# Sample retention states of a hybrid decoder layer: from TensorE matmuls on stacked split operands to element-wise passes on GpSimd

## The chip, the cores and the metric

The kernel runs on one core of a Trainium2 chip. The core has TensorE (PE in the profile, its weight loads PEld), VectorE (DVE), ScalarE (ACT), GpSimd (POOL) and SyncE (SP), which here only issues DMAs. Each engine takes its own instructions in the order in which they stand and waits on semaphores for the others. The metric is the device time of one launch in microseconds, as a median of several runs; lower is better.

## The reference, cut to what matters

One layer on 256 prompt tokens and, at the same time, 8 sequences of 8 sample tokens (320 columns in all). RMSNorm and an input projection feed an S5 head group and a retention head group; an output projection, a residual, a second norm and a SwiGLU feed-forward part of width 5632 follow. The change concerns one output of the retention group, the state of each sample sequence after its 8 tokens:

```python
def step(r, inp):
    qc, kc, vc = inp
    ...
    r_new = r * chunk_decay + jnp.einsum('bhmd,bhme->bhde', kc * k_decay, vc)
    return r_new, o
```

For the sample (`b` 8 sequences, `h` 8 heads, `m` 8 tokens, `d` and `e` 128 each) `r_new` is the old state times a scalar of the head plus the sum over 8 tokens of an outer product of a key (scaled by a power of the head's gamma) and a value. In all 64 states of 128x128 fp32, 512 KB per head. Nothing later in the layer reads them.

## The kernel before, in words

All activations lie transposed, features on the 128 partitions and the 320 tokens in columns. Weights are fp32 and are used in two parts: `wload` has SP load a chunk of 8 k-tiles (128x1024, 512 KB) into a tile `raw`, ACT casts it to `hi` (L131) and DVE subtracts, `lo = raw - hi` (L133). `gemm` then does three matmuls per k-tile: hi by x-hi (L143), hi by x-lo (L144), lo by x-hi (L145). Activations are split the same way.

The stages: a mixing stage (input projection, S5 scan, the eight retention heads, until about 340 us), the output projection and the GLU (until 488 us), then the feed-forward stage. That one runs `ffn_in(0)`, `ffn_in(1)`, `ffn_out(0)`, `ffn_in(2)`, `ffn_out(1)`, `ffn_in(3)`, `ffn_out(2)`, `ffn_out(3)`. Each `ffn_in` has 11 blocks (n = 0 to 43 in all) of two gemms of 16 k-tiles, `ps_fg` and `ps_fu`: four weight chunks a block. Behind them DVE scales both results, multiplies them (`fu<-fu,fg`) and makes `alo`.

Buffers: weights use the pool `wp` (3 `raw`, 3 `hi`, 3 `lo`) up to the first gemm of the feed-forward stage, after that `wp2` (4 `raw`, 3 `hi`, 3 `lo`). The state update takes its tiles from `wp`, under the same names, once the weights have left it.

Order: PE and POOL run in the order of the source (`tc.manual_schedule`). SP, ACT and DVE are ordered by the tile scheduler when the kernel is built; weight loads carry a high priority.

The state update before: in the mixing stage `head_k` transposes the sample's keys too and ACT stores them, scaled, in `kv[64:128]`; `head_v` stores the values in `kv[0:64]`. In the feed-forward stage `states_split` makes hi and lo parts of `kv` and stacks them by DMAs from ACT's queue; `states_load(h)` loads a head's old states and has DVE mask the values (`bmk`) so that one matmul serves four sequences; `states_add(h)` does two matmuls (`psu`, L1168) per head, DVE adds them to the scaled old state, and SP stores the result to `rs_o`.

Of the kernel before, what the change touches and what calls it, by code (L numbers as in the profile page):

```python
# [12 lines left out]
F32 = mybir.dt.float32  # L13
F32R = mybir.dt.float32r
# [3 lines left out]
ADD, SUB, MUL = ALU.add, ALU.subtract, ALU.mult  # L18
# [24 lines left out]

@with_exitstack
def hybrid_kernel(ctx, tc, xT, w_in, w_in4, w_out, w_glu, w_fi, w_fo, vecs, s5p, bc, x0,
                  r0, trig, masks, kdec, bmask, gq,
                  yT, s5p_o, s5s_o, rp_o, rs_o):
    nc = tc.nc
    pe, act, dve, pool, sp = nc.tensor, nc.scalar, nc.vector, nc.gpsimd, nc.sync
# [5 lines left out]
    def f(t):  # L55
        return t.bitcast(F32)
# [9 lines left out]
    bmk = cst.tile([P, 4], F32, name="bmk")  # L66

    kv = cst.tile([P, H, P], F32, name="kv")
# [32 lines left out]
    def mm(cost, *a, **k):  # L101
        pe.matmul(*a, **k)
        clk.now += cost

    def tr(out, in_):
        m = in_.shape[0]
        pe.transpose(out, in_, ident[:m, :m])
        clk.now += 0.12
# [68 lines left out]
    def tt(out, a, b, op):  # L177
        dve.tensor_tensor(out, a, b, op)  # L178
# [72 lines left out]
    kdc = mp.tile([P, H, 3], F32, name="kdc")  # L251
    gqt = mp.tile([P, H, NS], F32, name="gqt")
    retp = mp.tile([P, H, N], F32, name="retp")

# [462 lines left out]
    def head_k(h, q_, qg, k_, R):  # L717
        yield DL["k"]
        pst = misc("pst")
        for i, s in enumerate(STARTS):  # L720
            tr(pst[:, P * i:P * i + P], k_[:, s:s + P])
        kd = mp.tile([P, 2, P], F32, name="kd", tag="kd", bufs=1)
        with tc.high_priority(offset=EVAC):
            for i in range(2):
                act.mul(kd[:, i], pst[:, P * i:P * i + P], kdc[:, h, i:i + 1])
            act.mul(kv[64:128, h], pst[64:128, 2 * P:3 * P], kdc[64:128, h, 2:3])
        pss = misc("pss")
        mm(0.43, pss[:, 0:256], k_[:, 0:P], q_[:, 0:256], start=True, stop=True)
# [12 lines left out]

    def head_v(h, v_, qg, rt, R):
# [5 lines left out]
        with tc.high_priority(offset=EVAC):  # L748
            for i in range(3):
                act.mul(vT[:, i], pst2[:, P * i:P * i + P], rtok[:, i:i + 1])  # L750
        last = act.copy(kv[0:64, h], vT[64:128, 2])
        if h == 0:
            rot_t["values"] = last
            with tc.issue_after(last.ins):
# [10 lines left out]
        if h % 2:  # L765
            two = (HS[h - 1], R)
            for g in range(2):
                mm(0.11, po[64 * g:64 * g + 64, 2], smp[:, g], kv[0:64, h - 1 + g], start=True, stop=False,
                   tile_position=(0, 64 * g), skip_group_check=True)
# [103 lines left out]
    def do_k(h, ps=None):  # L873
        ps = proj(9 + 4 * h) if ps is None else ps
        R = HS[h]
        k_ = rot(ps, "k_")
        spawn(head_k(h, R["q_"], R["qg"], k_, R))
        run_due()

# [70 lines left out]
        k0 = k1  # L950
    ps0, ps1, pq, pk = accs
    for t_, s_ in ((x0t, x0), (csr, trig), (kdc, kdec),
                   (bmk, bmask), (gqt, gq)):
        sp.dma_start(t_, s_)
    for c in range(2):
        load_bc(c)
# [55 lines left out]
    def advance():  # L1012
        clk.now = max(clk.now, clk.heap[0][0])
        run_due()
# [52 lines left out]
        split_r(r4b[:, h - 4], h)  # L1067
    while clk.heap:
        advance()
    s5stack.close()  # L1070

    gl = ExitStack()
# [53 lines left out]
    def norm_ps(name):  # L1126
        return ps_n.tile([P, 512], F32, name=name, tag="n", bufs=2)
# [7 lines left out]

    SU = {}

    def states_split():  # L1140
        kvh, kvl = (wp.tile([P, 8, P], F32R, name=n, tag=n, bufs=3) for n in ("hi", "lo"))
        act.copy(kvh, kv)
        tt(kvl, kv, f(kvh), SUB)
        SU["k"] = [wp.tile([P, 8, P], F32R, name="hi", tag="hi", bufs=3) for _ in range(2)]
        SU["v"] = [wp.tile([P, 8, P], F32R, name="lo", tag="lo", bufs=3) for _ in range(2)]
        for i in range(2):
            for a in range(4):
                d = slice(32 * a, 32 * a + 32)
                act.dma_start(f(SU["k"][i][d]), f((kvh, kvl)[a // 2][64 + 32 * i:96 + 32 * i]))
                act.dma_start(f(SU["v"][i][d]), f((kvh, kvl)[a % 2][32 * i:32 * i + 32]))  # L1150

    def states_load(h):
        rt = wp.tile([P, NB, P], F32, name="raw", tag="raw", bufs=3)
        sp.dma_start(rt, r0[h])
        n = ("hi", "lo")[h % 2]
        vm = wp.tile([P, NB, P], F32R, name=n, tag=n, bufs=3)
        with tc.high_priority(offset=EVAC):
            for i in range(2):
                tt(vm[:, 4 * i:4 * i + 4], f(SU["v"][i][:, h]).unsqueeze(1).to_broadcast([P, 4, P]),
                   bmk.unsqueeze(2).to_broadcast([P, 4, P]), MUL)  # L1160
        SU[h] = rt, vm

    def states_add(h):
        rt, vm = SU.pop(h)
        for i in range(2):
            q = slice(4 * i, 4 * i + 4)
            ps = norm_ps("psu")
            pe.matmul(ps, SU["k"][i][:, h], vm[:, q].rearrange("p b e -> p (b e)"), start=True, stop=True)  # L1168
            stt(rt[:, q], rt[:, q], float(GAM[h] ** NS), ps.rearrange("p (b e) -> p b e", e=P), MUL, ADD)
        sp.dma_start(rs_o[h], rt)  # L1170

    def ffn_in(c):
        ahi = fp.tile([P, FCT, N], F32R, name="ahi", tag="ahi", bufs=2)
        alo = fp.tile([P, FCT, N], F32R, name="alo", tag="alo", bufs=2)
        for i in range(FCT):
            n = c * FCT + i
            if n == 0:
                spawn(ffn_norm(), DL["n2"])
            pg = gemm("ps_fg", w_fi[2 * n], KT, hhi, hlo)
            g = fp.tile([P, N], F32, name="fg", tag="fg", bufs=2)  # L1180
            tt(g, pg, rbc2, MUL)
            act.activation(g, g, AF.Silu)
            if n == 0:
                wpool[:] = [wp2, WP2]
            pu = gemm("ps_fu", w_fi[2 * n + 1], KT, hhi, hlo)
            u = fp.tile([P, N], F32, name="fu", tag="fu", bufs=2)
            tt(u, pu, rbc2, MUL)
            tt(u, u, g, MUL)
            act.copy(ahi[:, i], u)
            tt(alo[:, i], u, f(ahi[:, i]), SUB)  # L1190
            if c == 0:
                if i == 0:
                    states_split()
                if 3 <= i:
                    states_add(i - 3)
                if 2 <= i < 2 + H:
                    states_load(i - 2)
        return ahi, alo

    wp2 = ctx.enter_context(tc.tile_pool(name="wp2", bufs=1, reuse_waits="tile"))  # L1200
# [41 lines left out]
def _host(inp):  # L1242
# [58 lines left out]
    kd = np.zeros((P, H, 3))  # L1301
    for i in range(2):
        kd[:, :, i] = gam[None, :] ** (NP - 1 - (P * i + np.arange(P)[:, None])) * sc
    kd[64:, :, 2] = gam[None, :] ** (NS - 1 - (tt_[:, None] % 8)) * sc
    A["kdec"] = kd.astype(f)
    A["bmask"] = c((np.arange(P)[:, None] // 8 % 4 == np.arange(4)[None, :]).astype(f))
    A["gq"] = c(np.broadcast_to((gam[:, None] ** (np.arange(NS) + 1.0))[None], (P, H, NS)).astype(f))
    return A

# [25 lines left out]
```

## Time and profile before

| | |
|---|---|
| median of 3 runs | 1441.32 us (1441.31 to 1441.67) |
| span of the profiled execution | 1438.9 us |
| PE busy | 1425.4 us (99%) |
| DVE, ACT, POOL busy | 847.6, 600.2, 75.1 us |
| HBM read, written | 220.66 MB, 10.26 MB |
| granted TensorE clock, mean | 0.998 |

The span runs from the first to the last instruction of one profiled execution; the runs' times also hold what lies around it. Busy time of an engine is the union of its instructions, and a wait inside an instruction counts as busy. Matmuls are pipelined: a row of 0.31 us is issued every 0.15 us.

### The profile page before, as it was taken

To read this page: it belongs to the slowest core of one execution; us is meant where nothing else is said; L and a number is where in the kernel's file an instruction comes from. 1 tells how busy PE (TensorE), PEld (TensorE's weight loads), DVE (VectorE), ACT (ScalarE), POOL (GpSimd) and SP (SyncE) were. 2 spreads that over 40 slices of the span, in tenths; PEclk is the share of its full clock that TensorE was granted. 3 is DMA by queue.
4 is the path that set the end of the run, shared out by engine and by line. 5 is a ranking of instruction groups with operands and counts; after the bars stand their busy time and mean duration, and the time that the engine had idled before them with its cause. 6 is when DMAs were issued, how large, how long until landed. Compare 5 with 4: busy or idle time off the path is not lost.

```text
span 1438.9 us, 25723 instructions
## 1 busy us (share of the span) xinstructions
PE 1425.4 (99%) x10434; PEld 1411.7 (98%) x10434; DVE 847.6 (59%) x1378; ACT 600.2 (42%) x945; POOL 75.1 (5%) x161
## 2 busy tenths in 40 slices
PE   9999999999999999999999999999999999999997
PEld 8999999999999999999999999999999999999996
DVE  8978787777567655655444444454444444444454
ACT  7645555554355533333333333333333333333452
POOL 7610000000000000000000000000000000000001
PEclk9999999999999999999999999999999999999999
DMA  8555555556544666654444455444445444445443
GB/s 287 167 171 165 158 172 151 173 146 208 173 147 149 209 200 206 214 194 161 148 152 145 127 155 171 156 149 146 125 149 167 162 147 151 146 129 151 152 145 110
DMA packets 92774, 235.09 MB, mean 163 GB/s; under 512 B 26480, under 2 KB 40432, under 8 KB 92656
## 3 DMA queue, kind: packets, MB, share of 16 engines
q1 hardware_dynamic: 91744, 231.09, 50.7%
q10 hardware_dynamic: 912, 2.36, 0.6%
q8 instruction: 82, 1.34, 0.4%
q14 instruction: 36, 0.29, 0.1%
HBM read 220.66 MB, written 10.26 MB: 160 GB/s over the span
## 4 chain that ended last, share of the span: by engine, by line
PE 71%; DVE 1%; ACT 0%; issue 0%; DVEq 0%
PE ps_fo L144 7%; PE ps_fu L144 7%; PE ps_fu L145 7%; PE ps_fo L143 7%; PE ps_fu L143 7%; PE ps_fo L145 7%; PE ps_fg L143 7%; PE ps_fg L144 7%; PE ps_fg L145 7%; PE ps_o L144 1%; PE ps_o L143 1%; PE ps_o L145 1%; PE ps_g L144 1%; PE ps_g L145 1%; PE ps_g L143 1%; DVE x L178 0%
## 5 line engine op out<-in xcount | busy, mean ns | idle before, releaser
L133 DVE TENSOR_TENSOR lo<-raw,hi 128x1024 fp32r<-128x1024 f32 (+1 forms) x416 | 466.9, 1123 | 376.1 <-ACT hi L131 375.1
L131 ACT CAST hi<-raw 128x1024 fp32r<-128x1024 f32 (+1 forms) x416 | 402.0, 967 | 684.7 <-PE ps_fo L144 189.3
L143 PE MATMUL ps_fg<-hhi,hi 128*128 128x320 f32 x704 | 217.6, 309 | 0.0
L144 PE MATMUL ps_fo<-alo,hi 128*128 128x320 f32 x704 | 217.5, 309 | 0.0
L145 PE MATMUL ps_fo<-ahi,lo 128*128 128x320 f32 x704 | 217.5, 309 | 0.0
L143 PE MATMUL ps_fo<-ahi,hi 128*128 128x320 f32 x704 | 217.5, 309 | 0.0
L144 PE MATMUL ps_fg<-hlo,hi 128*128 128x320 f32 x704 | 217.4, 309 | 0.0
L144 PE MATMUL ps_fu<-hlo,hi 128*128 128x320 f32 x704 | 217.4, 309 | 0.0
L143 PE MATMUL ps_fu<-hhi,hi 128*128 128x320 f32 x704 | 217.4, 309 | 0.0
L145 PE MATMUL ps_fu<-hhi,lo 128*128 128x320 f32 x704 | 217.4, 309 | 0.0
L145 PE MATMUL ps_fg<-hhi,lo 128*128 128x320 f32 x704 | 217.4, 309 | 0.0
L143 PE MATMUL ps_p<-xhi,hi 128*128 128x320 f32 x560 | 177.8, 317 | 0.0
L145 PE MATMUL ps_p<-xhi,lo 128*128 128x320 f32 x560 | 173.3, 310 | 0.4 <-DVE lo L133 0.4
L144 PE MATMUL ps_p<-xlo,hi 128*128 128x320 f32 x560 | 172.9, 309 | 0.0
L144 PEld LDWEIGHTS ps_fg<-hlo,hi 128*128 128x128 f32 x704 | 132.4, 188 | 0.4
L143 PEld LDWEIGHTS ps_fg<-hhi,hi 128*128 128x128 f32 x704 | 132.3, 188 | 0.3
L143 PEld LDWEIGHTS ps_fu<-hhi,hi 128*128 128x128 f32 x704 | 132.4, 188 | 0.0
L144 PEld LDWEIGHTS ps_fu<-hlo,hi 128*128 128x128 f32 x704 | 132.4, 188 | 0.0
L145 PEld LDWEIGHTS ps_fu<-hhi,lo 128*128 128x128 f32 x704 | 132.4, 188 | 0.0
L145 PEld LDWEIGHTS ps_fg<-hhi,lo 128*128 128x128 f32 x704 | 132.3, 188 | 0.0
L143 PEld LDWEIGHTS ps_fo<-ahi,hi 128*128 128x128 f32 x704 | 132.2, 188 | 0.0
L144 PEld LDWEIGHTS ps_fo<-alo,hi 128*128 128x128 f32 x704 | 132.2, 188 | 0.0
(420 smaller groups left out, 1904.7 us busy)
## 6 DMA issues: line engine op xcount, KB each, us to landing
raw<-w_fi SPq DMA_DIRECT2D x176, 512.0 KB, 3.7
raw<-w_in SPq DMA_DIRECT2D x79, 512.0 KB, 4.1
raw<-w_fo SPq DMA_DIRECT2D x64, 512.0 KB, 3.5
raw<-w_out SPq DMA_DIRECT2D x32, 512.0 KB, 3.7
raw<-w_fo SPq DMA_DIRECT2D x64, 192.0 KB, 2.4
rt<-r SPq DMA_DIRECT2D x8, 512.0 KB, 5.4
raw<-w_glu SPq DMA_DIRECT2D x8, 512.0 KB, 3.4
raw<-r SPq DMA_DIRECT2D x8, 512.0 KB, 4.3
```

Of the source, the lines that this page charges most:

```text
L131: cast = act.copy(hi[:, :m], raw[:, :m])
L133: dve.tensor_tensor(lo[:, :m], raw[:, :m], f(hi[:, :m]), SUB)
L143: pe.matmul(ps, hi, xhi[:, k], start=k == 0, stop=False)
L144: pe.matmul(ps, hi, xlo[:, k], start=False, stop=False)
L145: pe.matmul(ps, lo, xhi[:, k], start=False, stop=k == nk - 1)
```

## The change

The sample's keys are no longer transposed. After each head's rotation POOL multiplies them by powers of gamma (`kdt`) into `kvf` (features on partitions, one column per token). The values stay token by token in `vs`, and eight DMAs at the end of the mixing stage write them to a DRAM tile `vd`, so that `vd[h, t]` is 8 sequences x 128 values of token t, 4 KB. The update is cut into 64 steps, one per head and token. A step loads `vd[h, t]` to all 128 partitions (`vb`, a 512 KB broadcast load into a buffer named `hi`), POOL multiplies it by the token's key column (`kvt`, named `lo`, 128x1024) and adds it to the state (named `raw`, 128x1024). Once per head POOL scales the state by a constant first. The source issues two steps per block of `ffn_in` from n = 2 on, with the load two steps ahead of its use.

```diff
@@ mixing stage
-        for i, s in enumerate(STARTS):
-            tr(pst[:, P * i:P * i + P], k_[:, s:s + P])
+        for i in range(2):
+            tr(pst[:, P * i:P * i + P], k_[:, P * i:P * i + P])
...
-            act.mul(kv[64:128, h], pst[64:128, 2 * P:3 * P], kdc[64:128, h, 2:3])
...
-        last = act.copy(kv[0:64, h], vT[64:128, 2])
+        last = act.copy(vs[:, h], vT[64:128, 2])
...
         k_ = rot(ps, "k_")
+        pool.tensor_tensor(kvf[:, h], k_[:, NP:N].rearrange("p (b t) -> p b t", t=NS),
+                           kdt[:, h].unsqueeze(1).to_broadcast([P, NB, NS]), MUL)
...
     while clk.heap:
         advance()
+    for b in range(NB):
+        sp.dma_start(vd[:, :, b].rearrange("h t e -> t h e"), vs[NS * b:NS * b + NS])
@@ feed-forward stage
-    def states_split():
...
-    def states_load(h):
...
-    def states_add(h):
...
+    SU = {"n": 0, "loads": []}
+
+    def states_load(j):
+
+        h, t = divmod(j, NS)
+        if t == 0:
+            SU["rt"] = wp.tile([P, NB, P], F32, name="raw", tag="raw", bufs=3)
+            sp.dma_start(SU["rt"], r0[h])
+        vb = wp.tile([P, NB, P], F32, name="hi", tag="hi", bufs=3)
+        sp.dma_start(vb, vd[h, t].unsqueeze(0).to_broadcast([P, NB, P]))
+        SU["loads"].append((h, t, vb, SU["rt"]))
+
+    def states_add():
+        h, t, vb, rt = SU["loads"].pop(0)
+        if t == 0:
+            pool.tensor_scalar(rt, rt, float(GAM[h] ** NS), None, MUL)
+        kvt = wp.tile([P, NB, P], F32, name="lo", tag="lo", bufs=3)
+        pool.tensor_tensor(kvt, vb, kvf[:, h, :, t].unsqueeze(2).to_broadcast([P, NB, P]), MUL)
+        pool.tensor_tensor(rt, rt, kvt, ADD)
+        if t == NS - 1:
+            sp.dma_start(rs_o[h], rt)
+
+    def states_step():
+        j = SU["n"]
+        SU["n"] += 1
+        if j < H * NS:
+            states_load(j)
+        if 2 <= j < H * NS + 2:
+            states_add()
...
-            if c == 0:
-                if i == 0:
-                    states_split()
-                if 3 <= i:
-                    states_add(i - 3)
-                if 2 <= i < 2 + H:
-                    states_load(i - 2)
+            if n >= 2:
+                states_step()
+                states_step()
```

How the scheduler orders SP's queue around it shows in the built programs. First SP in `ffn_in(0)` of the kernel before, a piece from the first state store on. `raw<-w_fi` is a weight chunk, `raw<-r0` a head's old states; in brackets are the engines or DMA queues that a row waits for.

```order
L1170 DMA rs_o<-raw_6810 128x1024 [waits DMAHW1_49,DVE_49]
L130 DMA raw_7169<-w_fi 128x1024 [waits DMAHW5_49,DMAHW2_49,DVE_49]
L1154 DMA raw_7236<-r0 128x1024 [waits DMAHW1_49]
L130 DMA raw_7241<-w_fi 128x1024 [waits DMAHW6_49,DVE_49]
L130 DMA raw_7247<-w_fi 128x1024 [waits DMAHW7_49,DVE_49]
L130 DMA raw_7305<-w_fi 128x1024 [waits DMAHW0_49,DVE_49]
L1170 DMA rs_o<-raw_6952 128x1024 [waits DVE_49]
```

There two state transfers of a head stand among four weight chunks, and all wait for DVE or DMA queues. The same engine in the changed kernel, from weight chunk 8 of the feed-forward stage (counted from 0) on; `hi<-vd` is a broadcast load:

```order
L130 DMA raw_6660<-w_fi 128x1024 [waits DMAHW6_49,DMAHW2_49,DVE_49]
L1152 DMA hi_6792<-vd_77 128x1024 [waits DMAHW3_49,PE_49]
L1152 DMA hi_6794<-vd_77 128x1024 [waits PE_49]
L130 DMA raw_6666<-w_fi 128x1024 [waits DMAHW7_49,DVE_49]
L1152 DMA hi_6926<-vd_77 128x1024 [waits PE_49]
L130 DMA raw_6724<-w_fi 128x1024 [waits DMAHW0_49,DVE_49]
L1152 DMA hi_6932<-vd_77 128x1024 [waits DMAHW3_49,Pool_49]
L130 DMA raw_6730<-w_fi 128x1024 [waits DMAHW1_49,DVE_49]
L1152 DMA hi_7067<-vd_77 128x1024 [waits DMAHW4_49,DMAHW2_49,Pool_49]
L130 DMA raw_6796<-w_fi 128x1024 [waits DVE_49]
```

From the fourth on, each broadcast load waits for POOL, and a weight load stands behind it; so it goes on to the 64th. The end of that piece on SP in the changed kernel, where the 64 loads run out:

```order
L1152 DMA hi_12665<-vd_77 128x1024 [waits DMAHW4_49,DMAHW2_49,Pool_49]
L130 DMA raw_8835<-w_fi 128x1024 [waits DVE_49]
L1152 DMA hi_12670<-vd_77 128x1024 [waits DMAHW6_49,Pool_49]
L130 DMA raw_8841<-w_fi 128x1024 [waits DMAHW5_49,DVE_49]
L130 DMA raw_8911<-w_fi 128x1024 [waits DMAHW7_49,DVE_49]
L1163 DMA rs_o<-raw_11487 128x1024 [waits Pool_49]
L130 DMA raw_8917<-w_fi 128x1024 [waits DMAHW1_49,DMAHW0_49,DVE_49]
```

The store of the last head stands two weight chunks behind the last broadcast load, before chunk 73; 62 weight loads stand between the first and the last of the 64. And POOL in the changed kernel at the start of the steps, where the kernel before has nothing between the last head's norm and the closing passes over `x1`:

```order
L1158 TENSOR_SCALAR raw_6790<-raw_6790 128x1024 [waits DMAHW4_49,DMAHW3_49,DMAHW5_49,DMAHW2_49,DMAHW6_49,DMAHW1_49,DMAHW7_49,DMAHW0_49,DVE_49]
L1160 TENSOR_TENSOR lo_6929<-hi_6792,kvf_74 128x1024 [waits DMAHW3_49,PE_49]
L1161 TENSOR_TENSOR raw_6790<-raw_6790,lo_6929 128x1024 [waits Pool_49]
L1160 TENSOR_TENSOR lo_6934<-hi_6794,kvf_74 128x1024 [waits DMAHW4_49,DVE_49,PE_49]
L1161 TENSOR_TENSOR raw_6790<-raw_6790,lo_6934 128x1024 [waits Pool_49]
```

Two passes of 128x1024 a step, 64 times, each addition behind its product. After the first few steps POOL waits only for the broadcast loads and its own results.

More of the change, by code (lines that the diff above doesn't have):

```diff
@@ L45, in hybrid_kernel @@
 def hybrid_kernel(ctx, tc, xT, w_in, w_in4, w_out, w_glu, w_fi, w_fo, vecs, s5p, bc, x0,
-                  r0, trig, masks, kdec, bmask, gq,
+                  r0, trig, masks, kdec, kdf, gq,
                   yT, s5p_o, s5s_o, rp_o, rs_o):
@@ L65, in hybrid_kernel @@
     vec = cst.tile([P, vecs.shape[1]], F32, name="vec")
-    bmk = cst.tile([P, 4], F32, name="bmk")
-    kv = cst.tile([P, H, P], F32, name="kv")
+    kvf = cst.tile([P, H, NB, NS], F32, name="kvf")
+    drs = ctx.enter_context(tc.tile_pool(name="drs", bufs=1, space=bass.MemoryType.DRAM))
+    vd = drs.tile([H, NS, NB, P], F32, name="vd")
     voff = {}
@@ L250, in hybrid_kernel @@
     csr = mp.tile([P, 2, N], F32, name="csr")
-    kdc = mp.tile([P, H, 3], F32, name="kdc")
+    kdc = mp.tile([P, H, 2], F32, name="kdc")
+    kdt = mp.tile([P, H, NS], F32, name="kdt")
+    vs = mp.tile([64, H, P], F32, name="vs")
     gqt = mp.tile([P, H, NS], F32, name="gqt")
@@ L767, in head_v @@
             for g in range(2):
-                mm(0.11, po[64 * g:64 * g + 64, 2], smp[:, g], kv[0:64, h - 1 + g], start=True, stop=False,
+                mm(0.11, po[64 * g:64 * g + 64, 2], smp[:, g], vs[:, h - 1 + g], start=True, stop=False,
                    tile_position=(0, 64 * g), skip_group_check=True)
@@ L952, in hybrid_kernel @@
     for t_, s_ in ((x0t, x0), (csr, trig), (kdc, kdec),
-                   (bmk, bmask), (gqt, gq)):
+                   (kdt, kdf), (gqt, gq)):
         sp.dma_start(t_, s_)
@@ L1133, in ffn_norm @@
         act.copy(rbc2, next(rg))
-    SU = {}
-    def states_split():
[L1141 to L1150, printed above, removed]
@@ L1152, in states_load @@
-    def states_load(h):
[L1153 to L1161, printed above, removed]
-    def states_add(h):
[L1164 to L1170, printed above, removed]
+    SU = {"n": 0, "loads": []}
@@ L1300, in _host @@
     A["masks"] = c(np.concatenate([mk, np.concatenate([sm, np.zeros_like(sm)], 1)], 2).astype(f))
-    kd = np.zeros((P, H, 3))
+    kd = np.zeros((P, H, 2))
     for i in range(2):
         kd[:, :, i] = gam[None, :] ** (NP - 1 - (P * i + np.arange(P)[:, None])) * sc
-    kd[64:, :, 2] = gam[None, :] ** (NS - 1 - (tt_[:, None] % 8)) * sc
     A["kdec"] = kd.astype(f)
-    A["bmask"] = c((np.arange(P)[:, None] // 8 % 4 == np.arange(4)[None, :]).astype(f))
+    A["kdf"] = c(np.broadcast_to((gam[:, None] ** (NS - 1.0 - np.arange(NS)) * sc)[None], (P, H, NS)).astype(f))
     A["gq"] = c(np.broadcast_to((gam[:, None] ** (np.arange(NS) + 1.0))[None], (P, H, NS)).astype(f))
```

## The prediction

> **What bounds the kernel now.** I read the page first (engine totals and the chain that ended last), then stretches of the feed-forward stage, then single rows of ACT, DVE and the queues there.
>
> ```profile
> span 1438.9 us, 25723 instructions
> PE 1425.4 (99%) x10434; PEld 1411.7 (98%) x10434; DVE 847.6 (59%) x1378; ACT 600.2 (42%) x945; POOL 75.1 (5%) x161
> PE 71%; DVE 1%; ACT 0%; issue 0%; DVEq 0%
> 660.00:810.00 150.00, 150.00 (x1024) 150.00 (x1024) 72.02 (x88) 53.21 (x65) 0.00 (x0) 1.00 0.45 144
> 1425.00:1438.00 13.00, 3.26 (x17) 2.38 (x16) 6.25 (x22) 0.43 (x1) 4.14 (x5) 0.78 0.51 202
> ```
>
> The last two are stretches: length, then busy time of PE, weight loads, DVE, ACT and POOL, granted clock, DMA share, GB/s. In the feed-forward stage PE never stops: 1024 matmuls in 150 us, 0.1465 us each. One weight chunk (8 k-tiles, 24 matmuls) is 3.516 us. POOL does nothing there, and DVE is half free.
>
> So only two things count: what leaves PE, and whether the weights still come every 3.516 us. A chunk comes by an SP load into `raw`, an ACT cast to `hi` and a DVE subtraction to `lo`:
>
> ```profile
> 659.35 1.05 ACT L131 CAST hi<-raw 128x1024 fp32r<-128x1024 f32 x1 [2.10 <-issue]
> 660.43 1.23 DVE L133 TENSOR_TENSOR lo<-raw,hi 128x1024 fp32r<-128x1024 f32 x1 [2.29 <-ACT hi L131]
> 663.50 0.49 DVE L178 TENSOR_TENSOR fu<-fu,fg 128x320 f32<-128x320 f32 x1
> 665.09 0.49 DVE L178 TENSOR_TENSOR alo<-fu,ahi 128x320 fp32r<-128x320 f32 x1
> raw<-w_fi SPq DMA_DIRECT2D x176, 512.0 KB, 3.7
> rt<-r SPq DMA_DIRECT2D x8, 512.0 KB, 5.4
> SPq L130 <- DVE lo L133: 973.4, 384, 7.5
> ```
>
> From issue to use that is 3.7 + 1.05 + 1.23 = 6.0 us. The last row is the queue's own: 384 times SP stood at a weight load until DVE had freed a `raw` buffer. SP runs ahead only as far as the buffers go, and whatever stands behind a waiting load waits too.
>
> **What PE is spared.**
>
> ```profile
> 546.62 0.46 PE psu L1168 x2
> 648.39 0.46 PE psu L1168 x2
> L107 PEld LDWEIGHTS pst<-ident,k__729 x3: 138/138/140, 52.5 to 52.8; 128*128 128x128 f32 x3
> 488.47 1.06 ACT hi L1142
> 489.55 1.23 DVE lo L178
> 491.35 0.31 PE L145 MATMUL ps_fg<-hhi,lo 128*128 128x320 f32 x1
> 491.79 0.80 PE L102 MATMUL ps_r<-ones,acc 128*128 128x1 f32 x6
> ```
>
> The first two rows are the first and last of eight such pairs on the chain: 8 x 0.46 = 3.7 us go. Of each head's three transposes of k one goes: 8 x 0.14 = 1.1 us. Between 491.50 (a matmul's 0.15 after the start of the row at 491.35) and 491.79 PE stands until the norm's sum is there, behind the cast and subtraction of `kv` (L1142 and after it, rows of the chain); 0.3 us go. Together 5.1 us. The DVE passes that go (masks and additions) and eight ACT multiplications are worth nothing: PE works through them.
>
> **What is added beside other work.** Eight small POOL products `kvf` in the mixing stage (POOL is busy 5% of the span) and eight stores to `vd` some 150 us ahead of their use: nothing, as long as POOL has room. `k_` has one buffer; were POOL full there, the next head's rotation would wait.
>
> **The 64 steps.** SP's order in the changed kernel decides. Its first two broadcast loads stand behind weight chunk 8 (counted from 0), and from the first to the last of the 64 there are only 62 weight loads: one `vb` per chunk, not one per two as the source reads. `vb` j goes into the buffer of `vb` j-3, so SP waits there until POOL has done product j-3, and the next weight load stands behind it. POOL's order has two passes of 128x1024 per step and waits for nothing on PE. So from a few steps on, one chunk comes per POOL step of T us. After the last `vb` come two more weight loads, then the store of head 7, which waits for POOL's very last addition, and behind it chunk 73.
>
> No row shows a POOL pass of that size. The nearest:
>
> ```profile
> L504 POOL TENSOR_TENSOR e<-e,ecs 128x128 f32<-128x128 f32 x1 | 0.4, 432 | 0.0
> L504 POOL TENSOR_TENSOR e<-e,ecs 128x256 f32<-128x256 f32 x1 | 0.6, 647 | 0.0
> L1236 POOL TENSOR_TENSOR x<-x,acc 128x320 f32<-128x320 f32 x5 | 4.1, 868 | 1101.9 <-ACT acc L1231 1101.9
> L325 POOL MEMSET d<- 128x512 f32 x2 | 1.0, 528 | 0.0
> L325 POOL MEMSET xp<- 128x640 f32 x2 | 1.2, 634 | 0.0
> ```
>
> The product has one repeated operand like L504, which grows by 215 ns per 128 columns: 647 + 6 x 215 = 1.94 us. The addition is in place on two full operands like L1236: in proportion 868 x 3.2 = 2.78 us, on the line through 128x128 2.47; I take 2.6, near the row of its own form. A pass thus lies between 1.94 and 2.78. The scaling, once in eight steps, has one input: 0.95 us at the memsets' slope, 2.6 as an addition; I take 1.3, an eighth of it 0.16.
>
> By the Trainium skill, GPSIMD Engine Reference, section 3.1, a two-input fp32 pass over 2048 columns takes 4497 ns; half of that, an estimate from that page, would be 2.25 a pass, and the sum below 1582 instead of 1585.
>
> Does POOL run freely beside DVE? Rows of the mixing stage:
>
> ```profile
> 59.11 1.21 DVE L133 TENSOR_TENSOR lo<-raw,hi 128x1024 fp32r<-128x1024 f32 x1
> 59.22 1.23 POOL L515 TENSOR_TENSOR tabl<-tabl,ta 128x32 f32<-128x32 f32 x1
> 61.10 0.27 POOL L518 TENSOR_TENSOR tabl<-tabl,ta 128x32 f32<-128x32 f32 x1
> 69.38 1.08 POOL L455 TENSOR_TENSOR scrt<-x0t,lp 128x256 f32<-128x256 f32 x1
> 69.89 1.65 DVE L133 TENSOR_TENSOR lo<-raw,hi 128x1024 fp32r<-128x1024 f32 x1
> 70.54 1.60 POOL L456 TENSOR_TENSOR lx<-scrt 128x256 f32<-128x256 f32 x1
> 71.46 1.22 DVE L178 TENSOR_TENSOR m<-raw_bc,lpc 128x512 f32<-128x512 f32 x1
> ```
>
> It doesn't. The same 128x32 POOL operation takes 0.27 us alone and 1.23 issued just after a `lo`. Then four in turn: `lo`, issued at 69.89, ends at 71.54, 1.08 after L455 ended; L456 ends at 72.14, 0.60 after `lo`; `m` at 72.68, 0.54 after L456. They take turns, each whole, and 1.23 - 1.08 = 0.15 of an operation's own time hides in the wait. For passes four times as wide no row shows it; I take it as the same.
>
> By the Trainium skill, SBUF — State Buffer, "Who interferes with whom", a DVE instruction with two SBUF inputs and a POOL instruction that reads SBUF exclude each other for the whole instruction, whatever its width; these rows agree at 256 columns.
>
> So while PE starves, each step holds POOL up by one `lo` (1.08) and half of the two small products per block of four chunks (0.49 - 0.15 = 0.34 each, 0.17 per step). Between dependent POOL operations lie 0.08 us (70.46 to 70.54 above).
>
> T = 1.94 + 2.6 + 0.16 + 0.08 + 1.08 + 0.17 = 6.03 us. Bounds: both passes 1.94 and the scaling 0.95, 5.33; both 2.78 and 2.6, 7.22.
>
> **The sum.**
>
> ```profile
> 497.17 0.31 PE L143 MATMUL ps_fu<-hhi,hi 128*128 128x320 f32 x1
> 497.47 1.23 DVE L133 TENSOR_TENSOR lo<-raw,hi 128x1024 fp32r<-128x1024 f32 x1 [0.29 <-ACT hi L131]
> ```
>
> PE began chunk 2 at 497.17, so chunk 73 is due at 497.17 + 71 x 3.516 = 746.8. The second row is `lo` of chunk 4; its end, 498.70, lets SP load chunk 8 and then `vb` 0, which lands 3.7 to 5.4 us later: POOL starts at about 503.4. It ends at 503.4 + 64T, and 6.0 us later chunk 73 is ready. The delay is 64T - 237.4. With 6.03 that is 148.5 us: span 1438.9 - 5.1 + 148.5 = 1582.3. The profiled span is 2.4 us under the median of the runs, 1441.3, so the time is 1585. The bounds of T give 1540 and 1661.
>
> **Rivals.**
> - *No exclusion between such wide passes.* T = 4.78, delay 68.5: 1505. Against it stand the rows above; for it, that they are narrower.
> - *The clock falls.* With T = 6.03 PE works 3.5 us and stands 2.5 in each step. The granted clock is 1.00 while PE is busy and 0.78 in the idle end (the stretch from 1425). At half clock a chunk takes 7.03 us and PE itself paces: from chunk 18, where the starving begins, to 72, 55 x 1.0 = 55 more: 1640. The Trainium skill, TensorE: Matmul & The Clock Gate, "What's actually happening", has the clock halved after an idle window of about 3.4 us; by that rule the 2.5 us stand would leave it full, while a T above 6.9 would not.
> - *The broadcast load is slow.* It reads one 4 KB row 128 times; no row shows such a load. The nearest of its size land in 3.7 and 5.4 us, and from the release of a buffer to its next use lie 2.5T = 15 us. Beyond that it paces: 20 us would make T 8 and the time 1711.
> - *Faster.* Were two-input passes as quick as memsets, 0.95 each, T would be 1.9 + 0.12 + 0.08 + 1.25 = 3.35, under a chunk's 3.516; SP would never be late and the 5.1 us stay: 1436. This decides below T = 3.71, where 64T is 237.4. Every two-input row above is dearer.
>
> **How the numbers follow.** The forecast (turns taken, T within its bounds) has 0.76, no exclusion 0.10, the falling clock 0.05, the slow load 0.05, the faster case 0.04. A range of 1500 to 1650 holds nearly all of the first and the next two; the two last and the uppermost end of T lie outside. Changes under 0.2% (2.9 us) can't be told from none: faster 0.04, within it 0.01 (T just at its turning point), slower 0.95.
>
> **What the next profile would show.** `psu` rows gone. PE solid until about 553 us: `vb` j lets chunk 8 + j be used at 493.3 + 6.03j, due at 518.3 + 3.516j, equal at j = 10. From there to about 895 PE busy for 3.516 of 6.03, digits of 5 or 6; the last 15 us of it one stop (the store of head 7); solid again after, with POOL idle. POOL busy about 75 + 64 x 6 = 455 us, since its rows count the wait for DVE. SP's longest waits at L1152 and on POOL. `lo` rows above 1.23 us while POOL works. Wrong: the passes' length above all, a microsecond per step moving the time by 64; then whether turns are taken; then SP not held where its order has it.

## The result, and the profile after

The changed kernel takes 1571.45 us (median; 1570.05 to 1573.48) against 1441.32 us: a ratio of 1.0902, 95% interval 1.0889 to 1.0915. The forecast was 1585 us, range 1500 to 1650.

The page of the kernel after: totals, then busy tenths in 40 slices of 39.3 us, then the chain that ended last by engine and by line.

```profile
span 1571.7 us, 25855 instructions
PE 1461.3 (93%) x10410; PEld 1432.2 (91%) x10410; DVE 964.4 (61%) x1345; ACT 597.2 (38%) x936; POOL 445.0 (28%) x305
PE   9999999999999976776878799999999999999997
POOL 7510010100000999999999200000000000000001
PEclk9999999999999998999989899999999999999999
...
PE 48%; POOL 23%; DMA 1%; DVE 1%; issue 0%; ACT 0%; SPq 0%; DVEq 0%; POOLq 0%; ACTq 0%
```

Counted from 0, TensorE now has a hole from slice 14 to slice 22, and POOL is solid from slice 13 to slice 21. POOL, which was not on the chain before, is 23% of it.

Two stretches of the same trace (length; busy time of PE, weight loads, DVE, ACT, POOL; granted clock; DMA share; GB/s):

```profile
600.00:700.00 100.00, 75.48 (x434) 71.01 (x433) 69.52 (x37) 22.66 (x27) 98.67 (x38) 0.91 0.66 217
900.00:1000.00 100.00, 100.00 (x684) 100.00 (x683) 46.60 (x61) 33.58 (x43) 0.00 (x0) 1.00 0.45 141
```

The matmuls have the same shape in both; the second is the end of `ffn_in(1)` and a part of `ffn_out(0)`. Beside POOL's steps there are 434 matmuls in 100 us, one chunk of 24 in 5.53 us; after them 684, one in 3.51.

Who holds the weights up is in SP's own queue, and what POOL does in its rows (minimum, median and maximum of a duration in ns, first and last start):

```profile
SPq L130 <- DVE lo L133: 778.0, 317, 7.5
SPq L1152 <- POOL lo L1160: 224.9, 54, 5.8
SPq L1163 <- POOL raw L1161: 69.4, 8, 17.3
```

```profile
L1160 POOL TENSOR_TENSOR lo<-hi,kvf x64: 1904/2897/2906, 510.0 to 870.1; 128x1024 f32<-128x1024 f32 x64
L1161 POOL TENSOR_TENSOR raw<-raw,lo x64: 2337/2520/3272, 512.7 to 872.1; 128x1024 f32<-128x1024 f32 x64
L1158 POOL TENSOR_SCALAR raw<-raw x8: 2768/3628/3748, 488.1 to 828.8; 128x1024 f32<-128x1024 f32 x8
```

The first row is no sign of trouble: the kernel before, whose TensorE never stops, has 973.4 us of it, SP running ahead of free buffers. The other two, waits for POOL, are new. SP stood 54 times at a broadcast load (L1152) until POOL had done a product, and 8 times at a store (L1163) until an addition was done. From the first addition's start to the last one's lie 872.1 - 512.7 = 359.4 us, 5.70 for each of 63 steps; this is T, the length of a POOL step. The broadcast loads of L1152 themselves, from issue to landing:

```profile
DMA to landing us min/median/max: 3.6/4.3/7.5
```

The groups of POOL's rows (busy us, mean ns of one) say of what a step is made:

```profile
L1161 POOL TENSOR_TENSOR raw<-raw,lo 128x1024 f32<-128x1024 f32 x64 | 169.8, 2653 | 5.0
L1160 POOL TENSOR_TENSOR lo<-hi,kvf 128x1024 f32<-128x1024 f32 x64 | 167.8, 2621 | 19.0 <-DMA hi<-vd 19.0
L1158 POOL TENSOR_SCALAR raw<-raw 128x1024 f32<-128x1024 f32 x8 | 27.1, 3392 | 158.0 <-DMA raw<-r 157.8
```

2.62 for a product, 2.65 for an addition and 27.1/64 = 0.42 for the scaling's share make 5.70 with unrounded means: POOL does nothing else in these 360 us.

The end of the stretch, in the chain of the kernel after (start, length, what):

```profile
872.06 2.35 POOL raw L1161
...
874.42 0.34 SPq L1163
...
874.87 5.11 DMA raw<-w_fi
...
880.08 1.05 ACT hi L131
...
881.15 1.24 DVE lo L133
```

The last addition ends, SP issues the store of head 7, and only then the weight load behind it; TensorE gets its chunk after another 5.11 + 1.05 us. Its row there (in brackets the idle time ahead of it):

```profile
881.18 0.63 PE L143 MATMUL ps_fg<-hhi,hi 128*128 128x320 f32 x1 [9.11 <-ACT hi L131]
```

### The profile page after: what moved, and what is told of

Read it like the earlier page. It is cut to its first block, busy times and chain, and to the rows that moved or that the text cites. A ratio compares the mean times of both kernels' runs of the same rounds, so it can differ in the third digit from the quotient of the medians.

```text
span 1571.7 us, 25855 instructions
## 1 busy us (share of the span) xinstructions
PE 1461.3 (93%) x10410; PEld 1432.2 (91%) x10410; DVE 964.4 (61%) x1345; ACT 597.2 (38%) x936; POOL 445.0 (28%) x305
## 4 chain that ended last, share of the span: by engine, by line
PE 48%; POOL 23%; DMA 1%; DVE 1%; issue 0%; ACT 0%; SPq 0%; DVEq 0%; POOLq 0%; ACTq 0%
POOL raw L1161 11%; POOL lo L1160 11%; PE ps_fo L145 7%; PE ps_fo L143 7%; PE ps_fo L144 7%; PE ps_fu L145 4%; PE ps_fu L143 4%; PE ps_fu L144 4%; PE ps_fg L145 4%; PE ps_fg L143 4%; PE ps_fg L144 4%; POOL raw L1158 2%; PE ps_o L143 1%; PE ps_o L144 1%; PE ps_o L145 1%; DMA raw<-w_fi 1%
## 5 line engine op out<-in xcount | busy, mean ns | idle before, releaser
L133 DVE TENSOR_TENSOR lo<-raw,hi 128x1024 fp32r<-128x1024 f32 (+1 forms) x416 | 556.9, 1339 | 436.2 <-ACT hi L131 435.8
L145 PE MATMUL ps_fu<-hhi,lo 128*128 128x320 f32 x704 | 224.4, 319 | 32.4 <-DVE lo L133 32.0
L145 PE MATMUL ps_fg<-hhi,lo 128*128 128x320 f32 x704 | 225.7, 321 | 28.3 <-DVE lo L133 28.3
L143 PE MATMUL ps_fg<-hhi,hi 128*128 128x320 f32 x704 | 224.7, 319 | 21.9 <-ACT hi L131 21.8
L143 PE MATMUL ps_fu<-hhi,hi 128*128 128x320 f32 x704 | 222.3, 316 | 10.4 <-ACT hi L131 10.4
L144 PE MATMUL ps_fg<-hlo,hi 128*128 128x320 f32 x704 | 223.2, 317 | 0.0
L1160 POOL TENSOR_TENSOR lo<-hi,kvf 128x1024 f32<-128x1024 f32 x64 | 167.8, 2621 | 19.0 <-DMA hi<-vd 19.0
L1161 POOL TENSOR_TENSOR raw<-raw,lo 128x1024 f32<-128x1024 f32 x64 | 169.8, 2653 | 5.0
L145 PEld LDWEIGHTS ps_fg<-hhi,lo 128*128 128x128 f32 x704 | 137.7, 196 | 33.8 <-DVE lo L133 33.8
L143 PEld LDWEIGHTS ps_fg<-hhi,hi 128*128 128x128 f32 x704 | 137.6, 196 | 23.8 <-ACT hi L131 23.7
L144 PEld LDWEIGHTS ps_fg<-hlo,hi 128*128 128x128 f32 x704 | 137.8, 196 | 0.0
```

The lines of the kernel that those rows point to most:

```text
L133: dve.tensor_tensor(lo[:, :m], raw[:, :m], f(hi[:, :m]), SUB)
L143: pe.matmul(ps, hi, xhi[:, k], start=k == 0, stop=False)
L144: pe.matmul(ps, hi, xlo[:, k], start=False, stop=False)
L145: pe.matmul(ps, lo, xhi[:, k], start=False, stop=k == nk - 1)
L1160: pool.tensor_tensor(kvt, vb, kvf[:, h, :, t].unsqueeze(2).to_broadcast([P, NB, P]), MUL)
L1161: pool.tensor_tensor(rt, rt, kvt, ADD)
```

## Experiments

The runs have labels, e1 to e11, which the expectations use too. The theory: SP issues in order, has one broadcast load for each weight chunk, and waits at each for POOL; so a chunk comes once in a POOL step. Rivals: A, POOL's passes shut VectorE out and its low parts come late; B, the traffic of the broadcast loads delays the weights; C, TensorE's falling clock.

### The floor: the states left out, and the passes narrowed

Run e3 leaves out the states; what remains is called the floor.

```diff
             if n >= 2:
-                states_step()
-                states_step()
+                pass
```

> Edit: the sample states are left out of the feed-forward stage altogether (no old states loaded, no broadcast loads, no POOL passes, no store of the sample states); the extra tiles of the mixing stage stay. Every theory: the floor. By the prediction's sum 1441.3 - 5.1 = 1436; by the trace after, in which the feed-forward stage begins at 495.79 instead of 491.79 us, 1441.3 - 5.1 + 4.0 = 1440. What e1 and e2 have above this run is what is left of the sample states' cost.

Measured: 1438.34 us, ratio 0.9978 (0.9969 to 0.9987).

Run e4 keeps all transfers and narrows POOL's passes to one of eight sequences.

```diff
-            pool.tensor_scalar(rt, rt, ...)
+            pool.tensor_scalar(rt[:, 0:1], rt[:, 0:1], ...)
-        pool.tensor_tensor(kvt, vb, kvf[:, h, :, t]...)
-        pool.tensor_tensor(rt, rt, kvt, ADD)
+        pool.tensor_tensor(kvt[:, 0:1], vb[:, 0:1], kvf[:, h, 0:1, t]...)
+        pool.tensor_tensor(rt[:, 0:1], rt[:, 0:1], kvt[:, 0:1], ADD)
```

> Edit: POOL's scaling, product and addition work on one of the eight sequences (128x128 instead of 128x1024), the other seven are stored as loaded; every load, store and place in SP's order is as in the changed kernel. Theory: POOL's step falls to about a fifth (two passes of some 0.3 to 0.5 us and gaps), below the 3.52 us of a weight chunk, so the waits for POOL end and the time is 1440, range 1436 to 1450. Rival B (traffic of 64 broadcast loads of 512 KB beside the weights): all bytes are still moved, one to a weight chunk, so most of the 130 us stays, 1500 or more. Rival A (exclusion) would fall away here too, so e1 and e2 tell A from the theory, and this run tells B.

Measured: 1438.26 us, ratio 0.9978 (0.9969 to 0.9988). A stretch of it, and one of POOL's groups:

```profile
600.00:700.00 100.00, 100.00 (x684) 100.00 (x683) 48.67 (x57) 35.86 (x43) 34.63 (x59) 1.00 0.94 330
```

```profile
L1161 POOL TENSOR_TENSOR raw<-raw,lo 128x128 f32<-128x128 f32 x64 | 34.0, 531 | 5.0
```

The DMA engines are 94% busy at 330 GB/s, more than the 217 of the kernel after, and TensorE does its full 684 matmuls. Rival B is out: all bytes are moved here, at no cost. Everything above 1438.3 us comes from the length of POOL's passes.

### The length of a step

Three runs shorten POOL's step. Run e5 halves the addition.

```diff
-        pool.tensor_tensor(rt, rt, kvt, ADD)
+        pool.tensor_tensor(rt[:, 0:4], rt[:, 0:4], kvt[:, 0:4], ADD)
```

> Edit: POOL's addition works on four of the eight sequences (128x512 instead of 128x1024), so the other four keep the scaled old state; everything else is as in the changed kernel. Theory (SP in order: one POOL step per weight chunk): the addition falls by about half of 2.34 to 2.65 us, a step by 1.2 to 1.3 us, to 4.4 to 4.5 us, still above 3.52, so the time falls by 64 x 1.2 to 1.3 = 77 to 83 us, to about 1491 (range 1480 to 1505). Rival A (VectorE shut out by POOL's passes sets the pace by itself): the passes shut out a quarter less, and with SP free e2 lost 58 us over the floor to it; the time would go to 1438 + 0.75 x 133 = 1538. Rival C (falling clock as an own term): the half-clock stretches of about 65 us would go as a whole once TensorE's stands get shorter, on top of the steps: 1470 or less.

Measured: 1499.53 us, ratio 1.0397 (1.0381 to 1.0413).

Run e11 leaves out the scaling.

```diff
-        if t == 0:
-            pool.tensor_scalar(rt, rt, float(GAM[h] ** NS), None, MUL)
```

> Edit: the eight scaling passes are left out (the old states are added to as loaded); loads, stores, products, additions and SP's order stay. It sizes the term that the prediction put at 0.16 us a step (64 x 0.16 = 10 us). Theory: seven of the eight passes lie in POOL's chain of steps (the first runs before it, at 488.1 us), 24.3 us together in the trace after, so the time is 1571.5 - 24 = 1547, range 1540 to 1554. Rival (the prediction's size of the term): 1571.5 - 10 = 1561. Rival A (the scaling's time is VectorE's turn taken, given back as waits of the passes beside it): 1565 or more.

Measured: 1552.75 us, ratio 1.0766 (1.0748 to 1.0784).

Run e10 leaves out the products.

```diff
-        kvt = wp.tile([P, NB, P], F32, name="lo", tag="lo", bufs=3)
-        pool.tensor_tensor(kvt, vb, kvf[:, h, :, t]..., MUL)
-        pool.tensor_tensor(rt, rt, kvt, ADD)
+        pool.tensor_tensor(rt, rt, vb, ADD)
```

> Edit: the products are left out; POOL scales the old states and adds the broadcast values to them as loaded, 64 additions of 128x1024; the loads, the stores and SP's order stay in kind, one broadcast load to a weight chunk. Theory (SP in order, the step against the 3.52 us of a weight chunk, turning point at 3.71 us by the prediction's line): a step is one addition of 2.4 to 2.7 us, 0.08 us of gap and 0.34 to 0.45 us for the scaling's share, 2.8 to 3.2 us, below the turning point, so the time is the floor plus little: 1440, range 1437 to 1450. Rival A (VectorE shut out sets the pace without SP): half of e2's passes at one to each weight chunk, so about half of its 58 us stay, 1467. Rival D (the time follows POOL's total work in a line without a turning point, 133 us for 364 us of steps): a step of 3.0 us is 53% of 5.69, so 1438 + 0.53 x 133 = 1508.

Measured: 1451.83 us, ratio 1.0063 (1.0046 to 1.0079).

The additions of the three, each in its own trace: half width, without scaling, and alone.

```profile
L1161 POOL TENSOR_TENSOR raw<-raw,lo x64: 1261/2141/2160, 510.9 to 794.8; 128x512 f32<-128x512 f32 x64
```

```profile
L1159 POOL TENSOR_TENSOR raw<-raw,lo x64: 2339/2523/3322, 508.5 to 849.8; 128x1024 f32<-128x1024 f32 x64
```

```profile
L1159 POOL TENSOR_TENSOR raw<-raw,hi x64: 2394/2644/3494, 507.7 to 745.6; 128x1024 f32<-128x1024 f32 x64
```

With the addition alone, this is TensorE's wait in the feed-forward stage (us in total, times, longest), and these are POOL's groups:

```profile
PE ps_fu L145 <- DVE lo L133: 9.6, 7, 2.1
```

```profile
L1159 POOL TENSOR_TENSOR raw<-raw,hi 128x1024 f32<-128x1024 f32 x64 | 182.4, 2851 | 52.3 <-DMA hi<-vd 48.5
L1158 POOL TENSOR_SCALAR raw<-raw 128x1024 f32<-128x1024 f32 x8 | 28.2, 3525 | 157.9 <-DVE lo L133 157.7
```

| kernel | T, last start minus first, by 63 | 64T - 237.4 | measured above 1438.3 |
|---|---|---|---|
| after | 5.70 | 127.7 | 133.1 |
| without scaling | 5.42 | 109.3 | 114.4 |
| half addition | 4.51 | 51.0 | 61.2 |
| addition alone | 3.78 | 4.3 | 13.5 |

The time follows the prediction's line from 5.70 to 4.51 us: 71.9 us less for 1.20 us of T, 60 to the microsecond where the line has 64, and 18.7 less for 0.29, 65 to the microsecond. So C is no term of its own while the steps last: the half addition's stretch has a granted clock of 0.97 instead of 0.91, and nothing beyond the step's shortening came back.

```profile
600.00:700.00 100.00, 86.18 (x539) 81.54 (x538) 67.12 (x45) 30.00 (x36) 98.20 (x49) 0.97 0.84 272
```

The half addition didn't become half as long (median 2.14 for 2.52 us: most of its rows hold a wait for VectorE), and the step still fell by 1.20, since the products waited less (2.30 in the mean for 2.62). The addition alone lies beyond the turning point: its passes and scalings take 182.4 + 28.2 = 210.6 us, 3.3 to a step, less than a chunk, and the 3.78 is the chunk's pace plus stops. It missed its range by 2 us. TensorE waited for VectorE alone there, seven times and 2.1 us at most. Behind the longest of these stops, which ends at 683.66, is this row:

```profile
680.23 3.38 DVE L133 TENSOR_TENSOR lo<-raw,hi 128x1024 fp32r<-128x1024 f32 x1
```

Its `hi` was ready by 678.65, and a low part takes 1.23 us undisturbed. That is rival A in small: neither its 1467 nor the line without a turning point (1508).

### SP's queue

Run e1 holds each pair of steps behind the last weight load of its block; `last_w` is a new one-element list.

```diff
-                sp.dma_start(raw[:, :m], src[:, k0:k0 + m])
+                last_w[0] = sp.dma_start(raw[:, :m], src[:, k0:k0 + m])
...
-                states_step()
-                states_step()
+                with tc.issue_after(last_w[0].ins):
+                    states_step()
+                    states_step()
```

> Edit: the loads, products and stores of the sample states are the same, but on SP each pair of broadcast loads is held behind the last weight load of its own block, so that two broadcast loads come to four weight loads (14.06 us of TensorE work) instead of one to one. Theory (SP in order waits for POOL at each broadcast load, one step of 5.69 us for one weight chunk of 3.52 us): a pair of steps takes 2 x 5.69 = 11.4 us and has 14.06 us, so SP no longer stops and TensorE runs through; 1441.3 - 5.1 (matmuls and transposes spared) + 4 (the feed-forward stage begins 4 us later than before) = 1440, range 1436 to 1448. Rival A (POOL's passes shut VectorE out, and VectorE's low parts come late for TensorE): POOL makes the same passes, so the time stays near 1571, with low parts above 2 us and TensorE waiting for them. Rival B (the broadcast loads' 33.5 MB delay the weights): the same bytes spread over twice the time, 1500 or more. Rival C (the halved clock alone): clock windows vanish only if TensorE's stands do, so this run does not tell C from the theory.

Measured: 1448.67 us, ratio 1.0047 (1.0032 to 1.0062), 0.7 us over the range. SP's and TensorE's waits, and a stretch:

```profile
SPq L1153 <- POOL lo L1161: 5.3, 6, 1.4
```

```profile
PE ps_fu L146 <- DVE lo L134: 6.7, 7, 1.0
```

```profile
600.00:700.00 100.00, 97.95 (x662) 96.90 (x661) 83.74 (x57) 34.13 (x41) 76.89 (x29) 1.00 0.66 230
```

The same 64 steps of the same passes, only two to four weight chunks: SP's 224.9 us of waiting at broadcast loads are 5.3, and 122.8 of the 133 us are gone. But the edit does two things: SP no longer stands, and POOL's passes lie further apart (busy 76.9 of 100 us instead of 98.7). So it rules out traffic and the passes' mere number, but does not part the theory from rival A; the next run does. Of the 10.3 us left, 6.7 are seven stops of TensorE for a low part; two of them, which end at 631.9 and 689.8 us, come right behind stretches in which POOL worked without a gap from 609.1 and 666.9 us on.

Run e2 issues the transfers of the states from POOL's own queue.

```diff
-            sp.dma_start(SU["rt"], r0[h])
+            pool.dma_start(SU["rt"], r0[h])
-        sp.dma_start(vb, vd[h, t]...)
+        pool.dma_start(vb, vd[h, t]...)
-            sp.dma_start(rs_o[h], rt)
+            pool.dma_start(rs_o[h], rt)
```

> Edit: the broadcast loads, the loads of the old states and the stores of the new ones are issued from POOL's own queue; SP carries weights alone. Theory: POOL now waits for itself only, SP never stands behind it: 1440, range 1436 to 1450, with POOL's steps closer to each other than one to a weight chunk or not, without effect on TensorE; what the issues cost on POOL lengthens POOL's stretch alone. Rival A (exclusion of VectorE by POOL's passes): still near 1571, TensorE waiting on low parts. Rival B (traffic): 64 broadcast loads at the same or a higher rate, still 1500 or more.

Measured: 1496.55 us, ratio 1.0382 (1.0366 to 1.0397). The theory had 1440. A stretch, TensorE's longest wait in sum, and three VectorE operations by their durations in ns:

```profile
600.00:700.00 100.00, 85.71 (x568) 83.08 (x567) 99.71 (x48) 28.97 (x36) 97.81 (x55) 1.00 0.69 228
```

```profile
PE ps_fu L145 <- DVE lo L133: 40.6, 33, 2.0
```

```profile
L178 DVE TENSOR_TENSOR fg<-ps_fg,rbc x21: 475/478/480, 514.8 to 845.7; 128x320 f32<-128x320 f32 x21
L178 DVE TENSOR_TENSOR fu<-fu,fg x22: 494/1692/2445, 504.4 to 849.9; 128x320 f32<-128x320 f32 x22
L178 DVE TENSOR_TENSOR alo<-fu,ahi x22: 2197/2200/2694, 509.0 to 854.5; 128x320 fp32r<-128x320 f32 x22
```

SP is free of POOL here, and the chunks come at 568 matmuls per 100 us instead of 434; but VectorE shows 99.7 of 100 us busy with 48 instructions, since its rows count the time for which POOL holds it up. The operation with one input in PSUM takes its 0.48 us as ever; the two of the same width with both inputs in SBUF take 1.69 and 2.20 in the median, where they took 0.49 before the change. So freeing SP alone takes 74.9 of the 133 us back, with POOL as dense as before; 58 stay. That is rival A, true in kind: a second limit behind the first. POOL's passes packed without a gap leave VectorE too few turns, and TensorE waits for low parts. Whether it is the passes or the issues on POOL, the next run, e7, tells; its edit is that of this run and the narrow passes above together.

> Edit: as in e2 all loads and stores of the sample states are issued from POOL's queue, and as in e4 POOL's passes work on one of eight sequences (128x128). It tells what cost e2 its 58 us over the floor. If it is the passes (VectorE cannot start its own two-input instructions on SBUF while a POOL pass of 1.9 to 2.9 us runs, is 99.8 of 100 us busy or held, and TensorE waits for low parts): the passes here take 0.5 to 0.6 us, the time is the floor, 1438 to 1441. If it is the issue on POOL (80 issues of 0.58 us) or the traffic of this queue: 1460 to 1496.

Measured: 1439.88 us, ratio 0.9984 (0.9975 to 0.9993). Beside narrow passes the issues and the queue cost 1 to 2 us at most; so the 58 us of the run before belong to the passes.

### The last store

Run e6 moves the store of the last head.

```diff
-        if t == NS - 1:
+        if t == NS - 1 and h < H - 1:
             sp.dma_start(rs_o[h], rt)
+        SU["end"] = rt
...
     ffn_out(0, a0)
+    sp.dma_start(rs_o[H - 1], SU["end"])
```

> Edit: only the store of head 7's states is moved, from its place in SP's queue during the feed-forward stage to one after the first output part of that stage; the 64 broadcast loads stay where they are. Theory: the stop of 9.1 us at 871.5 to 881.2 us, in which SP waits for the last addition with a weight load behind it, goes or shrinks to the weight chunk's own chain: 1571.5 - 9 = 1562, range 1559 to 1567. Rival: the last broadcast loads stand there too and hold SP just as long: 1571.

Measured: 1556.84 us, ratio 1.0795 (1.0781 to 1.0810), 14.6 under the kernel after. It isn't the clean test it was meant to be: at that place of the program the steps had reached head 4 (not 5, as the next expectation says), the moved line stored head 4's tile, early, and head 7's states weren't stored. So a second run, e9, holds the right store behind a late weight load; it keeps the first piece above and sets `last_w` as in e1:

```diff
     a3 = ffn_in(3)
+    with tc.issue_after(last_w[0].ins):
+        sp.dma_start(rs_o[H - 1], SU["end"])
```

> Edit: head 7's store alone is held behind the last weight load of the stage's fourth input part, so that it leaves its place in SP's queue (behind the last broadcast loads); the 64 broadcast loads, the other seven stores and their places stay. (In e6 the scheduler took the moved line early, with head 5's tile, and head 7's states were not stored at all.) Theory: of the stop of 9.1 us at 871.5 to 881.2 us the part goes that SP spends at the store, and the last weight loads go out as soon as their own buffers are free: 1571.5 - 9 = 1562, range 1556 to 1567. Rival: the last broadcast loads hold SP just as long, 1571.

Measured: 1559.65 us, ratio 1.0817 (1.0801 to 1.0833), 11.8 less than the kernel after. Its stretch at the end of POOL's work, and the same of the kernel after:

```profile
870.00:900.00 30.00, 29.14 (x199) 28.88 (x198) 17.36 (x19) 10.78 (x13) 1.43 (x1) 1.00 0.48 158
```

```profile
870.00:900.00 30.00, 20.53 (x128) 19.86 (x127) 11.56 (x14) 8.52 (x10) 4.32 (x3) 0.83 0.55 193
```

TensorE's stop is gone from it: 71 matmuls more, which at 0.1465 us each are 10.4 us of work. That is the stop of 9.1 us and the slow start behind it, at a granted clock of 0.83 in the stretch instead of 1.00. The cause of the last 1.4 us stays open.

### The steps spread out

Run e8 spreads the steps, one to a block.

```diff
             if n >= 2:
-                states_step()
-                states_step()
+                with tc.issue_after(last_w[0].ins):
+                    states_step()
...
+            if c < FCH - 1 and n % 2:
+                with tc.issue_after(last_w[0].ins):
+                    states_step()
             tt(x1[:, n], x1[:, n], ps, ADD)
```

The first piece is in `ffn_in`, the second in `ffn_out`; `last_w` is set as above.

> Edit: as e1, but one step (one broadcast load, one product, one addition) to a block of four weight loads in place of two, and 24 of the 66 steps to every second of the first 48 blocks of the output part; each broadcast load behind the last weight load of its block. Theory: a step of 5.5 us has 14 us (10 us in the output part), SP does not wait, and VectorE is shut out by two passes only before it has a free stretch to catch up, where e1 had seven stops of 1.0 to 1.3 us at the third pass or later: floor of e3 plus little, 1438 to 1442, not slower than the kernel before. Rival A (each step costs TensorE a stop of its own of 0.2 us or more): 1438 + 64 x 0.2 = 1451 or more.

Measured: 1439.36 us, ratio 0.9981 (0.9972 to 0.9990), 1 us above the floor. A stretch, and all that TensorE waited for low parts in the feed-forward stage:

```profile
600.00:700.00 100.00, 100.00 (x684) 100.00 (x683) 69.70 (x57) 35.94 (x43) 35.20 (x15) 1.00 0.60 198
```

```profile
PE ps_fo L146 <- DVE lo L134: 0.9, 1, 0.9
```

The whole work of the change is in it, and it is as fast as a kernel without the states to within 1 us. Against the kernel before it gains 0.19%, just about what can be told from none.

## Why the prediction was right, point by point

**One broadcast load per weight chunk, and SP waiting in order.** Right, and it carries the result: with the passes unchanged and only their loads' places in SP's order moved, 122.8 of 133 us went (e1). Freeing SP without spreading the passes takes 74.9 of them (e2); the rest needs the passes apart as well.

**A chunk per step of T.** Right: the line 64T - 237.4 gives 127.7 for the measured T, and 133.1 were measured above the floor. **T itself** was 0.33 us too large, 6.03 for 5.70. Rows of the kernel after show its terms free of VectorE (the last two) and beside it (the first two):

```profile
863.87 2.89 POOL L1160 TENSOR_TENSOR lo<-hi,kvf 128x1024 f32<-128x1024 f32 x1
866.85 3.26 POOL L1161 TENSOR_TENSOR raw<-raw,lo 128x1024 f32<-128x1024 f32 x1
870.07 1.92 POOL L1160 TENSOR_TENSOR lo<-hi,kvf 128x1024 f32<-128x1024 f32 x1
872.06 2.34 POOL L1161 TENSOR_TENSOR raw<-raw,lo 128x1024 f32<-128x1024 f32 x1
```

The product was put at 1.94 and took 1.90 to 1.92 alone. The addition was put at 2.6, between the proportion and the line: 2.34, below both. The scaling was the term most mis-sized: 1.3 us forecast, at least 2.77 and 3.39 in the mean; without it the time fell by 18.7 us, not 10. By itself it takes 2.77/8 = 0.35 a step instead of 0.16. So an error of -0.26 (the addition) and one of +0.19 (the scaling) largely cancelled, which is luck; VectorE's turns were a little shorter (2.62 - 1.90, 2.65 - 2.34 and 0.62/8 make 1.11, not 1.25), and the gaps of 0.08 lie within the rows' overlap. By the Trainium skill, GPSIMD Engine Reference, section 3.1, the estimate was 2.25 a pass: the two measured ones, 1.90 and 2.34, lie on both sides of it.

**Turns taken.** Right at four times the width that the rows before showed: a product beside VectorE's low part takes 2.89 instead of 1.92 us. The rival without exclusion (1505) is out. The Trainium skill, SBUF — State Buffer, "Who interferes with whom", has a VectorE instruction with two SBUF inputs shut out by a POOL instruction that reads SBUF, and one with a single SBUF input, outside its two-port modes, not: e2's rows, 1.69 and 2.20 against 0.48 us, agree.

But the prediction counted the turns only as POOL's loss. What VectorE loses it left out: nothing here, where SP holds TensorE back more, and 58 us where SP doesn't (e2). Who takes the first limit away finds this one.

**Start and end.** POOL's first product was forecast at 503.4 us and began at 510.0: the first broadcast load took 7.5 us to land, not 3.7 to 5.4, and the stage itself began late. Its end was forecast at 889.3 and came at 874.4. These 14.9 us nearly make the 13.6 by which the time was over-forecast, and they are two errors: T 0.33 too large is 64 x 0.33 = 21 us, and the late start took 6.6 of them back. That the forecast came so near is in part luck. The last stop was forecast at 15 us, and is 9.1; moving its store is worth 11.8.

**What TensorE is spared.** Forecast 5.1 us; the floor runs are 3.5 us under the kernel before. The 3.7 us of `psu` fit that; the 1.4 of transposes and norm don't show. **Beside other work, nothing:** right to about that 1.6 us. The trace after begins the feed-forward stage at 495.6 us instead of 491.8, from which the expectation of e1 and e3 took a loss of 4 us; in e4, with the same code up to there, it begins at 491.6:

```profile
L102 PE MATMUL ps_r<-ones,acc x12: 164/250/251, 495.6 to 1556.2; 128*128 128x1 f32 x12
```

```profile
L102 PE MATMUL ps_r<-ones,acc x12: 164/250/250, 491.6 to 1420.1; 128*128 128x1 f32 x12
```

All eleven variants, which share that code, begin it between 490.9 and 493.7 us. So most of these 4 us belong to that one execution, and the expectations of 1440 for the floor were 1.7 too high.

**Busy shares.** TensorE was forecast to be solid until about 553 us, and its first stop ends at 545.2; POOL busy was put at 455 us and is 445.0. PE's digits were forecast at 5 or 6 and are 6 to 8. 434 matmuls of 0.1465 us would be 64 us in 100; 75.5 are shown, at a mean granted clock of 0.91: the clock fell, which was a rival, but POOL set the pace all the same, and the slower matmuls filled time in which TensorE would have stood.

**The other rivals.** The broadcast load was not slow (4.3 us in the median). A pass of less than a chunk, the faster case, was not near: it takes T under 3.71; the additions and scalings alone come to 3.3 (e10), and a product adds at least 1.90.

## What to carry to other kernels

Where a queue issues in order, a load that waits for a slow engine sets the pace of all loads behind it: count how many of them stand between two weight loads, and compare the slow engine's step with the work that these weights feed, not its total with the span. Holding such loads behind a weight load, which also spread POOL's passes, took 123 of 133 us back here with a few lines. After that, long POOL passes are best kept apart from each other, since VectorE's two-input work gets its turn only between them.

## What the runs showed of the hardware that was not expected

**The clock falls after stops shorter than 3.4 us.** In the kernel after, the granted clock goes from full to half and back in steps, 11 times each way between 560 and 890 us. The 18 of these changes that can be timed to 0.01 us lie on one grid of 3.413 us. Two pieces of that grid; the granted clock is the third number from the right:

```profile
605.20:608.61 3.41, 1.63 (x9) 1.10 (x8) 2.31 (x1) 2.28 (x3) 3.33 (x3) 1.00 0.90 310
608.61:612.02 3.41, 3.18 (x12) 3.18 (x13) 3.37 (x3) 0.36 (x2) 3.33 (x2) 0.50 0.56 192
612.02:615.43 3.41, 3.41 (x25) 3.41 (x24) 3.38 (x3) 1.34 (x2) 3.41 (x2) 1.00 0.72 255
```

```profile
625.69:629.10 3.41, 1.01 (x6) 0.47 (x4) 0.71 (x1) 1.42 (x2) 3.33 (x3) 1.00 0.36 145
629.10:632.51 3.41, 2.23 (x8) 2.23 (x9) 1.12 (x1) 0.00 (x0) 3.33 (x3) 0.50 0.81 275
```

TensorE worked for 1.63 us of the first window, with no stop longer than 1.96 us, and still ran the next one at half clock, with 12 matmuls; 1.01 us of work in another had the same effect. Of this trace's windows at full clock, the 11 with at most 1.63 us of work are followed by half clock and all those with 1.66 or more by full clock. So about half a window of work decides, not the length of one stop; the traces of e5, e6, e9 and e11 put the border between 1.6 and 1.9 us.

By the Trainium skill, TensorE: Matmul & The Clock Gate, "What's actually happening", an idle window of about 3.4 us drops the clock to half. The length agrees with the grid, but here windows with work in them were enough. The prediction had judged by the length of a single stop and kept the clock at 1.00.

**A scaling on POOL is dearer than an addition.** 128x1024 in place with one input and a constant takes at least 2.77 us, with two inputs at least 2.34.
